# The gate and up projections of a feed-forward layer, token-major in blocks of 512 columns

## The chip, the cores and the metric

The kernel runs on one core of one Trainium2 chip. The metric is the device time of one execution in microseconds; the time before is the median of three runs.

## The reference

One decoder layer on 256 tokens of width 2,048 in float32. The two feed-forwards are what the change is about:

```python
def swiglu(x, w_gate, w_up, w_down):
    return (jax.nn.silu(x @ w_gate) * (x @ w_up)) @ w_down

x = x + 0.5 * swiglu(rms_norm(x, ffn1_norm), ffn1_w_gate, ffn1_w_up, ffn1_w_down)
...                                   # the token mixing, between the two
x = x + 0.5 * swiglu(rms_norm(x, ffn2_norm), ffn2_w_gate, ffn2_w_up, ffn2_w_down)
```

Gate and up weights are 2,048 x 5,632, down weights 5,632 x 2,048. `rms_norm` divides each token by the root of its mean square and multiplies by a gain per feature.

## The kernel before, in words

**Numbers in two halves.** A float32 value is used as a high part, rounded to the matmul's format (`whi`, `XH`), and a remainder (`wlo`, `XL`). A product is three terms: high x high, high x remainder, remainder x high.

**Weight tiles.** All weights come as tiles of 128 x 1,024 elements, 512 KB, one transfer each, through four `raw` buffers on SyncE's queue (`ensure_dma`, L286). ScalarE makes the high part (`split_hi`, L303), VectorE the remainder (`split_lo`, L322), each into four buffers, three tiles ahead of TensorE. A raw buffer is free, and the next transfer starts, when the remainder is made.

**Units.** A `Unit` is one bank pair of results: its tiles, the matmuls of half a tile (`emit`), and what follows (`done`). There are two forms. `unit_a` (L353) is feature-major: the weights are the stationary operand, 256 output columns, four 128-row slices of the contraction per tile. For each 128 columns it streams high and remainder of the activations together (512 columns) and then the high part alone (256), 16 matmuls to a tile. `unit_b` (L341) is token-major: the activations are the stationary operand, 512 output columns, two slices per tile, 12 matmuls of 512 columns. In the kernel before only the mixing stage uses `unit_b`.

**Feed-forward before.** `ffn` (L456) makes 22 gate units and 22 up units of 256 columns, alternating, then the down units, which read `H`, the product in two halves, feature-major. The normalisation's scale per token, R, is not known when the first units begin, since the gain alone is put into `XH` and `XL`; so the first two gates and ups are stored and scaled in jobs that wait for R. Each result leaves its bank by `fold` (a ScalarE copy and a VectorE addition); the gate is multiplied by R in a row (`RB`) and goes through Silu; the product with up is cast and its remainder taken.

**Order.** All engines run in the order written. Two units fit in the banks at once. Small work is in generators, the jobs: after each half tile `step` (L216) runs the jobs that are ready by a clock of estimated costs (`Estimate`), and `force` (L263) writes out the rest of a job at once. The main loop is at L1258.

**Opening.** The first gate and the first up unit are interleaved tile by tile. Their tiles share the x slices, which are loaded, scaled and split (`x_load`, `x_part`) just ahead of use; the first tile goes in pieces (`PIECES`).

Of the kernel before, what the change touches and what calls it, by code (L numbers as in the profile page):

```python
# [9 lines left out]
F32 = mybir.dt.float32  # L10
# [3 lines left out]
AF = mybir.ActivationFunctionType  # L14
# [4 lines left out]
S = 256  # L19
D = 2048  # L20
FF = 5632
EPS = 1e-6
NEG = -1e30
KD = D // 128
# [1 line left out]
NB = 4  # L26
NRAW = 4
LAG = 4.0
PIECES = ((0, 1), (1, 2), (2, 4))
SPREAD = ("ca", "R0", "R1", "R2")  # L30
MARGIN = 0.3

# [82 lines left out]
def layer(ctx: ExitStack, tc: tile.TileContext, xt, cols, w_small, b_in,  # L115
          wg1, wu1, wd1, w_in, cw1k, cw2k, cw1v, cw2v, wb_n, wb_m, w_out, wg2, wu2, wd2, out):
    nc = tc.nc
    est = Estimate()
    V, A, T, G = (Engine(e, n, est) for e, n in ((nc.vector, "V"), (nc.scalar, "A"), (nc.tensor, "T"), (nc.gpsimd, "G")))
# [10 lines left out]
    def nm(p):  # L130
        uid[0] += 1
        return f"{p}{uid[0]}"
# [20 lines left out]
    XH, XL = XX[:, :, 0, :], XX[:, :, 1, :]  # L153
# [29 lines left out]
    cur = {}  # L183
# [7 lines left out]
    def job(gen, name=None, need=(), rank=0):  # L191
        jobs.append([est.end, gen, name, need, rank])
        jobs.sort(key=lambda j: j[4])
# [69 lines left out]
    def force(name):  # L263
        settle()
        while name not in past:
            j = next(j for j in jobs if j[2] == name)
            for n in j[3]:
                force(n)
            if step(j):
                uptake(j)  # L270
# [15 lines left out]
    def ensure_dma(n):  # L286
        while state["dma"] <= min(n, len(tiles) - 1):
            i = state["dma"]
            src, nk, ncol = tiles[i]
            r = st.tile([128, nk, ncol], F32, name=nm("raw"), tag="raw", bufs=NRAW)  # L290
            est.q["D"] = max(est.q["D"], done_at.pop(i - NRAW, 0.0)) + 1.45
            if i == 0:
                for a, b in PIECES:
                    x_load(a, b)
                    nc.sync.dma_start(r[:, a:b, :], src[:, a:b, :])
            else:
                if i in (2, 4, 6):
                    x_load(2 * i, 2 * i + 4)
                nc.sync.dma_start(r, src)
            raws[i] = r, est.q["D"] + 2.0  # L300
            state["dma"] += 1
# [38 lines left out]

    def unit_b(w, c0, H, L, kts, done, pre=None):  # L341

# [10 lines left out]
    def unit_a(w, c0, ncol, kts, act, done, pre=None):  # L353

        nk = 1024 // ncol

        def emit(ps, h, e, wh, wl):
            a = act()
            for k in range(e * nk // 2, (e + 1) * nk // 2):
                kt = nk * h + k  # L360
                for c in range(ncol // 128):
                    cs = slice(c * 128, c * 128 + 128)
                    mul(ps[:, c, :], wh[:, k, cs], a[:, kt].rearrange("p a t -> p (a t)"), start=kt == 0, stop=False)
                for c in range(ncol // 128):
                    cs = slice(c * 128, c * 128 + 128)
                    mul(ps[:, c, 0:S], wl[:, k, cs], a[:, kt, 0, :], start=False, stop=kt == kts - 1)
        return Unit(blocks(w, c0, ncol, kts), emit, done, pre)
# [22 lines left out]
    def fold(o, ps, c=2):  # L390

        A.copy(o, ps[:, 0:c, S:])
        V.tensor_add(o, ps[:, 0:c, 0:S], o)

    units = []
# [56 lines left out]
    def rb2():  # L452
        return RB[:, None, :].to_broadcast([128, 2, S])


    def ffn(wg, wu, wd, first, nxt, name):  # L456


        env = {}

        def open_pool():
            p = tc.tile_pool(name=nm("ffn"), bufs=1)
            env["pool"] = p
            env["p"] = cur["ffn"] = p.__enter__()
            env["H"] = env["p"].tile([128, KF, 2, S], F32R, name=nm("H"), tag="h")

        def close_pool():
            env["pool"].__exit__(None, None, None)

        def gate_done(c):  # L470
            def f(ps):
                if c in (2, 3):
                    force(first + "up%d" % (c - 2))
                g = env["p"].tile([128, 2, S], F32, name=nm("sg"), tag="sg", bufs=2)
                fold(g, ps)
                env["g", c] = g
                if c < 2:
                    job(later(gate, c), first + "gate%d" % c, (first,))
                else:
                    gate(c)  # L480
            return f

        def gate(c):
            g = env["g", c]
            V.tensor_mul(g, g, rb2())
            A.activation(g, g, AF.Silu)

        def up_done(c):
            def f(ps):
                h = env["p"].tile([128, 2, S], F32, name=nm("sh"), tag="sh", bufs=2)  # L490
                fold(h, ps)
                env["h", c] = h
                if c < 2:
                    job(later(up, c), first + "up%d" % c, (first + "gate%d" % c,))
                else:
                    up(c)
            return f

        def up(c):
            h = env["h", c]  # L500
            V.tensor_mul(h, h, env["g", c])
            H = env["H"][:, 2 * c:2 * c + 2]
            A.copy(H[:, :, 0, :], h)
            V.tensor_sub(H[:, :, 1, :], h, H[:, :, 0, :].bitcast(F32))

        def later(f, c):
            yield
            f(c)

        def down_done(c):  # L510
            return lambda ps: residual(env["p"], c, ps, True, nxt, name)

        for c in range(FF // 256):
            units.append(unit_a(wg, c * 256, 256, KD, the_x, gate_done(c), open_pool if c == 0 else None))
            units.append(unit_a(wu, c * 256, 256, KD, the_x, up_done(c)))
        for c in range(D // 256 - (nxt is None)):
            units.append(unit_a(wd, c * 256, 256, KF, lambda: env["H"], down_done(c)))
        if nxt is None:
            units.append(unit_last(wd, D - 256, 256, KF, lambda: env["H"], lambda ps, k: store_last(env["p"], ps, k)))
        return close_pool  # L520
# [655 lines left out]
    close1 = ffn(wg1, wu1, wd1, "R0", C_GM, "R1")  # L1176
    close_mix = mixing()
    n = len(units)
    close2 = ffn(wg2, wu2, wd2, "R2", None, None)
    first2 = units[n].pre  # L1180

    def pre2():
# [1 line left out]
        first2()  # L1184
    units[n].pre = pre2

    units[0].guest, units[0].between = units.pop(1), (1, 3, 5, 7)
    plan = []
    for u in units:
        order = [u] * len(u.tiles)  # L1190
# [10 lines left out]
    x_at = {}  # L1201
    xv = xt.rearrange("(k p) t -> p k t", p=128)

    def x_load(a, b):
        nc.sync.dma_start(X[:, a:b, :], xv[:, a:b, :])  # L1205
        est.q["D"] += 0.36 * (b - a)
        for kt in range(a, b):
            x_at[kt] = est.q["D"] + 2.0
# [11 lines left out]
    for t in range(2):  # L1220
        G.affine_select(mcb[:, t, :], mcb[:, t, :], [[-16, 32]], OP.is_ge, NEG, base=128 * t - 31, channel_multiplier=1)
        G.affine_select(m01[:, t, :], m01[:, t, :], [[-16, 32]], OP.is_ge, 0.0, base=128 * t - 31, channel_multiplier=1)

    def x_part(a, b):
        est.after(x_at[a])
        for kt in range(a, b):
            A.activation(XH[:, kt, :], X[:, kt, :], AF.Identity, scale=col(C_G1 + kt))
            V.scalar_tensor_tensor(XL[:, kt, :], X[:, kt, :], col(C_G1 + kt), XH[:, kt, :].bitcast(F32),
                                   op0=OP.mult, op1=OP.subtract)

    def g_start():
        for a in range(8):
            yield
            v = X[:, 2 * a:2 * a + 2, :]
            if a == 0:
                A.activation(acc, v, AF.Square)
            else:
                sq = cur["ffn"].tile([128, 2, S], F32, name=nm("sq"), tag="y", bufs=2)
                A.activation(sq, v, AF.Square)
                V.tensor_add(acc, acc, sq)  # L1240
            yield
        yield from g_r()

    def open_x():
        ensure_split(0)
        ensure_split(1)
        x_part(4, 8)
        ensure_split(2)
    first = units[0].pre

# [8 lines left out]
    for h, (u, i) in enumerate(plan):  # L1259
        if i == 0:  # L1260
            if u.pre:
                u.pre()
            banks[u] = (u.bank or psA)()
        ps = banks[u]
        if h in (1, 3):
            x_part(6 + 2 * h, 10 + 2 * h)
        wh, wl, t, _ = splits.pop(h)
        est.q["T"] = max(est.q["T"], t)
        for e in range(2):
            u.emit(ps, i, e, wh, wl)  # L1270
            late = None if small_ones else cur.get("late")
            j = step()
            (split_lo if e else split_hi)(h + NB - 1)
            if u.mid and not e and i == len(u.tiles) - 1:
                est.after(est.q["T"] + 0.1)
                u.mid(ps)
            if e and i == len(u.tiles) - 1:
                del banks[u]
                est.after(est.q["T"] + 0.1)
                u.done(ps)  # L1280
            if late and late is cur.get("late"):
                settle()
            if j:
                uptake(j)
# [61 lines left out]
```

## Time and profile before

| | |
|---|---|
| median of 3 runs | 2225.91 us (2225.1 to 2227.18) |
| the profiled execution | 2226.1 us, its span 2224.4 us |
| TensorE busy | 2211.5 us (99%) |
| VectorE busy | 1373.9 us (62%) |
| ScalarE busy | 1104.7 us (50%) |
| mean transfer rate | 185 GB/s |

The span is the part between the first and the last instruction. Busy shares are means over the span. Matmuls overlap in the records, so the pace of the stream is read from the starts of matmuls, not from their lengths.

### The profile page before, as it was taken

The page shows a single profiled execution, that of the slowest core. Times are in us where ns is not written, and L with a number is a line of the kernel's source. Part 1 is how long each engine was busy: PE and PEld are TensorE (multiplying, and loading weights), DVE is VectorE, ACT ScalarE, POOL GpSimd, SP SyncE. Part 2 cuts the span into 40 slices and gives each one's busy share as a digit, 9 for nine tenths or more (in the row PEclk, how much of TensorE's full clock was granted, in tenths as well). Part 3 has the DMA queues.
Part 4 walks back from the last instruction along what each step waited for, and adds up shares of the span by engine and source line. Part 5 has one row for each costly group of instructions (what it writes and reads, how often), then busy time and mean ns, then how long its engine had stood idle before and what let it go on. Part 6 is the DMA issues. An engine that isn't in the chain of part 4 may idle for free.

```text
span 2224.4 us, 31821 instructions
## 1 busy us (share of the span) xinstructions
PE 2211.5 (99%) x12649; PEld 1913.9 (86%) x12649; DVE 1373.9 (62%) x1719; ACT 1104.7 (50%) x1471; POOL 27.8 (1%) x54
## 2 busy tenths in 40 slices
PE   8999999999999999999999999999999999999999
PEld 7888888888888888777888888888888888888888
DVE  7655555555555678876777666765555555555553
ACT  6444444444444465666774544554444444443332
POOL 0000000000000000001100000000000000000000
PEclk9999999999999999999999999999999999999999
DMA  7666666666655776544556666566666666666663
GB/s 248 184 192 187 188 192 186 188 190 193 189 181 185 201 229 192 162 131 122 155 170 189 189 189 188 182 190 183 189 188 189 189 189 190 189 199 199 199 197 126
DMA packets 395078, 412.59 MB, mean 185 GB/s; under 512 B 13296, under 2 KB 375920, under 8 KB 394928
## 3 DMA queue, kind: packets, MB, share of 16 engines
q1 hardware_dynamic: 394064, 408.08, 59.5%
q0 software_dynamic: 720, 2.36, 0.4%
q8 instruction: 99, 1.62, 0.3%
q14 instruction: 51, 0.42, 0.1%
q10 hardware_dynamic: 144, 0.11, 0.0%
HBM read 408.40 MB, written 2.10 MB: 185 GB/s over the span
## 4 chain that ended last, share of the span: by engine, by line
PE 98%; DVE 1%; DMA 0%; ACT 0%; issue 0%; SPq 0%; DVEq 0%; ACTq 0%
PE mm L110 94%; PE sc L110 2%; PE tr L110 2%; DVE wlo L110 0%; DMA raw<-in_wg_dram 0%; DMA raw<-in_w_in_dram 0%; DVE nx L110 0%; DVE t L110 0%; DVE y L110 0%; ACT t L110 0%; ACT whi L110 0%; ACT kk L110 0%; DVE mo L110 0%; SPq L1205 0%; DVE rt L110 0%
## 5 line engine op out<-in xcount | busy, mean ns | idle before, releaser
L110 DVE TENSOR_TENSOR wlo<-raw,whi 128x1024 fp32r<-128x1024 f32 (+1 forms) x772 | 929.8, 1224 | 558.0 <-ACT whi L110 555.3
L110 PE MATMUL mm<-XX,whi 128*128 128x512 f32 x3600 | 1137.5, 397 | 5.7 <-DVE XX L110 4.7
L110 ACT CAST whi<-raw 128x1024 fp32r<-128x1024 f32 (+1 forms) x772 | 792.8, 1046 | 555.8 <-PE mm L110 444.2
L110 PEld LDWEIGHTS mm<-XX,wlo 128*128 128x128 f32 x3600 | 676.9, 188 | 161.0 <-DVE wlo L110 2.2
L110 PE MATMUL mm<-XX,wlo 128*128 128x256 f32 x3600 | 710.4, 278 | 0.3 <-DVE wlo L110 0.2
L110 PEld LDWEIGHTS mm<-XX,whi 128*128 128x128 f32 x3600 | 550.6, 189 | 7.3 <-ACT whi L110 6.0
L110 PE MATMUL mm<-H,whi 128*128 128x512 f32 (+1 forms) x1496 | 446.4, 382 | 0.5 <-DVE y L110 0.5
L110 PEld LDWEIGHTS mm<-H,wlo 128*128 128x128 f32 x1408 | 264.9, 188 | 58.6
L110 PE MATMUL mm<-H,wlo 128*128 128x256 f32 x1408 | 284.2, 278 | 0.0
L110 PEld LDWEIGHTS mm<-H,whi 128*128 128x128 f32 x1496 | 228.3, 189 | 0.7 <-DVE y L110 0.7
L110 PE MATMUL mm<-whi,XX 128*128 128x512 f32 x576 | 191.5, 399 | 0.0
L110 PEld LDWEIGHTS mm<-whi,XX 128*128 128x128 f32 x576 | 108.4, 188 | 21.7 <-issue 0.7
L110 PE MATMUL mm<-wlo,XX 128*128 128x512 f32 x288 | 113.7, 395 | 0.2 <-DVE wlo L110 0.2
L110 PE MATMUL mm<-M__10703,whi 128*128 128x512 f32 x256 | 79.8, 393 | 0.0
L110 ACT COPY sg<-mm 128x512 f32<-128x512 f32 x44 | 25.8, 587 | 84.3 <-PE mm L110 84.3
L110 ACT COPY sh<-mm 128x512 f32<-128x512 f32 x44 | 25.8, 587 | 82.8 <-PE mm L110 82.8
L110 DVE TENSOR_TENSOR sg<-mm,sg 128x512 f32<-128x512 f32 x44 | 30.4, 692 | 54.7 <-ACT sg L110 54.5
L110 DVE TENSOR_TENSOR sh<-mm,sh 128x512 f32<-128x512 f32 x44 | 30.4, 692 | 54.5 <-ACT sh L110 54.5
L110 PEld LDWEIGHTS mm<-wlo,XX 128*128 128x128 f32 x288 | 54.3, 189 | 9.9 <-DVE wlo L110 0.6
L110 ACT CAST H<-sh 128x512 fp32r<-128x512 f32 x44 | 27.3, 620 | 62.3 <-DVE sh L110 62.3
L110 ACT ACTIVATE sg<-sg 128x512 f32<-128x512 f32 x44 | 27.8, 632 | 60.2 <-DVE sg L110 60.2
L110 PEld LDWEIGHTS mm<-M__10703,wlo 128*128 128x128 f32 x256 | 48.1, 188 | 10.9
(190 smaller groups left out, 1185.6 us busy)
## 6 DMA issues: line engine op xcount, KB each, us to landing
raw<-in_wu_dram SPq DMA_DIRECT2D x176, 512.0 KB, 4.7
raw<-in_wd_dram SPq DMA_DIRECT2D x176, 512.0 KB, 4.5
raw<-in_wg_dram SPq DMA_DIRECT2D x175, 512.0 KB, 4.7
raw<-in_w_in_dram SPq DMA_DIRECT2D x168, 512.0 KB, 4.5
raw<-in_w_out_dram SPq DMA_DIRECT2D x32, 512.0 KB, 4.7
raw<-in_wb_n_dram SPq DMA_DIRECT2D x16, 512.0 KB, 5.2
raw<-in_wb_m_dram SPq DMA_DIRECT2D x16, 512.0 KB, 4.3
bias<-in_b_in_dram POOLq DMA_DIRECT2D x9, 256.0 KB, 3.8
```

The source lines that it names most:

```text
L110: return g(out, *a, **k)
```

## The change

Gate and up use `unit_b` with 512 columns, 11 units each, eight tiles to a unit. Results are token-major, so R is a scalar per partition: Silu reads the bank directly and scales there. VectorE multiplies the up bank by the gate into `h`. Then a job (`g_turn`) turns `h` to feature-major with 16 transposes of 32 x 32 blocks in four groups (`turn`), and the cast and the remainder write `H`. A job must be over before the next gate is taken from its bank; the last one is forced out with the second-last tile of the first down unit. The first pair is copied out of its banks unscaled and scaled in place when R is known. In the opening, x is loaded and split two slices at a time, and the units interleave over 16 tiles.

```diff
-PIECES = ((0, 1), (1, 2), (2, 4))
+PIECES = ((0, 1), (1, 2))
...
-                if i in (2, 4, 6):
-                    x_load(2 * i, 2 * i + 4)
+                if i in range(2, KD, 2):
+                    x_load(i, i + 2)
...
+    def turn(o, h, j):
+
+        ov_ = o.rearrange("p k (t q f) -> p t k q f", t=2, f=32)
+        hv = h.rearrange("p t (k q f) -> p t k q f", q=4, f=32)
+        for i in range(4):
+            V.transpose(ov_[32 * j:32 * j + 32, :, :, i, :], hv[32 * i:32 * i + 32, :, :, j, :])
...
         def gate_done(c):
             def f(ps):
-                if c in (2, 3):
-                    force(first + "up%d" % (c - 2))
-                g = env["p"].tile([128, 2, S], F32, name=nm("sg"), tag="sg", bufs=2)
-                fold(g, ps)
-                env["g", c] = g
-                if c < 2:
-                    job(later(gate, c), first + "gate%d" % c, (first,))
+                if c == 1:
+                    force(first + "up")
+                if c:
+                    force(name + "h%d" % (c - 1))
+                g = env["g", c] = env["p"].tile([128, 2, 512], F32, name=nm("sg"), tag="sg", bufs=1)
+                if c:
+                    gate(g, ps)
                 else:
-                    gate(c)
+                    A.copy(g, ps)
+                    job(later(gate, g, g), first + "gate", (first,))
             return f
...
-        def gate(c):
-            g = env["g", c]
-            V.tensor_mul(g, g, rb2())
-            A.activation(g, g, AF.Silu)
+        def gate(g, src):
+            for t in range(2):
+                A.activation(g[:, t, :], src[:, t, :], AF.Silu, scale=cur["R"][:, t:t + 1])
...
         def up_done(c):
             def f(ps):
-                h = env["p"].tile([128, 2, S], F32, name=nm("sh"), tag="sh", bufs=2)
-                fold(h, ps)
-                env["h", c] = h
-                if c < 2:
-                    job(later(up, c), first + "up%d" % c, (first + "gate%d" % c,))
+                h = env["p"].tile([128, 2, 512], F32, name=nm("sh"), tag="sh", bufs=1)
+                if c:
+                    up(c, h, ps)
                 else:
-                    up(c)
+                    A.copy(h, ps)
+                    job(later(up, c, h, h), first + "up", (first + "gate",))
             return f
...
-        def up(c):
-            h = env["h", c]
-            V.tensor_mul(h, h, env["g", c])
-            H = env["H"][:, 2 * c:2 * c + 2]
-            A.copy(H[:, :, 0, :], h)
-            V.tensor_sub(H[:, :, 1, :], h, H[:, :, 0, :].bitcast(F32))
+        def up(c, h, src):
+            V.tensor_mul(h, src, env["g", c])
+            job(g_turn(c, h), name + "h%d" % c)
+
+        def g_turn(c, h):
+
+            ht = env["p"].tile([128, 4, S], F32, name=nm("ht"), tag="sg", bufs=1)
+            H = env["H"][:, 4 * c:4 * c + 4]
+            for j in range(4):
+                yield
+                turn(ht, h, j)
+                yield
+            yield
+            A.copy(H[:, :, 0, :], ht)
+            V.tensor_sub(H[:, :, 1, :], ht, H[:, :, 0, :].bitcast(F32))
+            yield
...
-        for c in range(FF // 256):
-            units.append(unit_a(wg, c * 256, 256, KD, the_x, gate_done(c), open_pool if c == 0 else None))
-            units.append(unit_a(wu, c * 256, 256, KD, the_x, up_done(c)))
+        for c in range(FF // 512):
+            units.append(unit_b(wg, c * 512, XH, XL, KD, gate_done(c), None if c else open_pool))
+            units.append(unit_b(wu, c * 512, XH, XL, KD, up_done(c)))
...
-    units[0].guest, units[0].between = units.pop(1), (1, 3, 5, 7)
+    units[0].guest, units[0].between = units.pop(1), range(1, KD, 2)
...
-        x_part(4, 8)
+        x_part(2, 4)
...
-        if h in (1, 3):
-            x_part(6 + 2 * h, 10 + 2 * h)
+        if h in range(1, KD - 4, 2):
+            x_part(h + 3, h + 5)
```

The rest of the diff passes the second feed-forward a name for its jobs and lets the sum of squares of x (`g_start`) wait until its slices have been split.

## Rows read from the trace of the kernel before

**Rows 1.** The page, parts 1 and 2: busy time, clock in 40 slices.
```profile
PE 2211.5 (99%) x12649; PEld 1913.9 (86%) x12649; DVE 1373.9 (62%) x1719; ACT 1104.7 (50%) x1471; POOL 27.8 (1%) x54
...
PEclk9999999999999999999999999999999999999999
```
**Rows 2.** The page, part 4: the chain of waits, share by engine.
```profile
PE 98%; DVE 1%; DMA 0%; ACT 0%; issue 0%; SPq 0%; DVEq 0%; ACTq 0%
```
**Rows 3.** Timeline of TensorE in gate and up: start us, us, engine, what.
```profile
300.12 0.63 PE L110 MATMUL mm<-XX,whi 128*128 128x512 f32 x2
300.59 0.40 PE L110 MATMUL mm<-XX,wlo 128*128 128x256 f32 x2
...
311.27 0.62 PE L110 MATMUL mm<-XX,whi 128*128 128x512 f32 x2
```
**Rows 4.** Timeline of TensorE in the mixing stage, token-major form.
```profile
786.01 0.62 PE L110 MATMUL mm<-whi,XX 128*128 128x512 f32 x2
786.46 0.39 PE L110 MATMUL mm<-wlo,XX 128*128 128x512 f32 x1
...
797.57 0.62 PE L110 MATMUL mm<-whi,XX 128*128 128x512 f32 x2
```
**Rows 5.** Timeline of the first 22 us.
```profile
4.67 1.19 PE L110 MATMUL mm<-XX,whi 128*128 128x512 f32 x2 [4.67 <-DVE XX L110]
...
8.15 0.62 ACT L110 CAST whi<-raw 128x512 fp32r<-128x512 f32 x1 [1.19 <-DMA raw<-in_wg_dram]
...
10.28 1.04 ACT L110 CAST whi<-raw 128x1024 fp32r<-128x1024 f32 x1 [1.51 <-DMA raw<-in_wu_dram]
...
18.00 0.62 PE L110 MATMUL mm<-XX,whi 128*128 128x512 f32 x2
```
**Rows 6.** The chain of waits up to 60 us: start us, us, what.
```profile
43.48 0.34 PE sc L110 x4
...
49.95 0.44 PE sc L110 x4
```
**Rows 7.** Timeline of TensorE at the end of the first gate and up stage.
```profile
501.46 0.63 PE L110 MATMUL mm<-H,whi 128*128 128x512 f32 x2
```
**Rows 8.** Busy time in two stretches; the last columns are clock, DMA share, GB/s.
```profile
0.00:20.00 20.00, 14.24 (x60) 11.23 (x61) 11.29 (x19) 13.69 (x24) 2.53 (x18) 1.00 0.91 298
100.00:500.00 400.00, 400.00 (x2299) 349.01 (x2298) 234.58 (x234) 187.53 (x216) 0.00 (x0) 1.00 0.61 189
```
**Rows 9.** Groups of ScalarE by shape: busy us, mean ns, idle before.
```profile
L110 ACT CAST whi<-raw 128x1024 fp32r<-128x1024 f32 x769 | 791.4, 1048 | 554.7 <-PE mm L110 444.2 <-ACT whi L110 69.5 <-issue 22.4
...
L110 ACT ACTIVATE sg<-sg 128x512 f32<-128x512 f32 x44 | 27.8, 632 | 60.2 <-DVE sg L110 60.2
L110 ACT CAST H<-sh 128x512 fp32r<-128x512 f32 x44 | 27.3, 620 | 62.3 <-DVE sh L110 62.3
L110 ACT COPY sh<-mm 128x512 f32<-128x512 f32 x44 | 25.8, 587 | 82.8 <-PE mm L110 82.8
```
**Rows 10.** Groups of VectorE by shape, the same columns.
```profile
L110 DVE TENSOR_TENSOR wlo<-raw,whi 128x1024 fp32r<-128x1024 f32 x769 | 928.3, 1227 | 556.7 <-ACT whi L110 554.0 <-PE mm L110 1.9
...
L110 DVE TENSOR_TENSOR H<-sh,H 128x512 fp32r<-128x512 f32 x44 | 30.5, 693 | 30.2 <-ACT H L110 30.2
...
L110 DVE TENSOR_TENSOR vcz<-sc,mask 128x1024 f32<-128x1024 f32 x1 | 1.2, 1225 | 1.7 <-PE sc L110 1.7
...
L110 DVE COPY t<-tr 128x256 f32<-128x256 f32 x2 | 0.7, 415 | 0.0
L110 DVE TENSOR_TENSOR_SCAN t<-t,t 4x256 f32<-4x256 f32 x1 | 0.7, 680 | 0.1
```
**Rows 11.** Timeline of one tile's cast and remainder in gate and up.
```profile
309.19 1.05 ACT L110 CAST whi<-raw 128x1024 fp32r<-128x1024 f32 x1 [1.73 <-PE mm L110]
...
310.27 1.23 DVE L110 TENSOR_TENSOR wlo<-raw,whi 128x1024 fp32r<-128x1024 f32 x1 [1.55 <-ACT whi L110]
```
**Rows 12.** The chain of waits from 840 to 900 us.
```profile
866.49 2.36 DVE wlo L110 x2
868.87 4.61 DMA raw<-in_w_in_dram
```

More of the change, by code (lines that the diff above doesn't have):

```diff
@@ L506, in later @@
-        def later(f, c):
-            yield
-            f(c)
+                h = env["p"].tile([128, 2, 512], F32, name=nm("sh"), tag="sh", bufs=1)
+                if c:
+                    up(c, h, ps)
+                else:
+                    A.copy(h, ps)
+                    job(later(up, c, h, h), first + "up", (first + "gate",))
+            return f
+        def up(c, h, src):
[8 more added lines that the diff above has]
+                yield
+            yield
+            A.copy(H[:, :, 0, :], ht)
+            V.tensor_sub(H[:, :, 1, :], ht, H[:, :, 0, :].bitcast(F32))
+            yield
@@ L510, in down_done, with later, turned, f @@
+        def later(f, *a):
+            yield
+            f(*a)
+        def turned(u):
+            emit = u.emit
+            def f(ps, h, e, wh, wl):
+                if h == len(u.tiles) - 2:
+                    force(name + "h%d" % (FF // 512 - 1))
+                emit(ps, h, e, wh, wl)
+            u.emit = f
+            return u
         def down_done(c):
             return lambda ps: residual(env["p"], c, ps, True, nxt, name)
-        for c in range(FF // 256):
-            units.append(unit_a(wg, c * 256, 256, KD, the_x, gate_done(c), open_pool if c == 0 else None))
-            units.append(unit_a(wu, c * 256, 256, KD, the_x, up_done(c)))
+        for c in range(FF // 512):
+            units.append(unit_b(wg, c * 512, XH, XL, KD, gate_done(c), None if c else open_pool))
+            units.append(unit_b(wu, c * 512, XH, XL, KD, up_done(c)))
@@ L516, in ffn @@
         for c in range(D // 256 - (nxt is None)):
             units.append(unit_a(wd, c * 256, 256, KF, lambda: env["H"], down_done(c)))
+            if c == 0:
+                turned(units[-1])
         if nxt is None:
@@ L1178, in layer @@
     n = len(units)
-    close2 = ffn(wg2, wu2, wd2, "R2", None, None)
+    close2 = ffn(wg2, wu2, wd2, "R2", None, "R3")
     first2 = units[n].pre
@@ L1222, in layer @@
         G.affine_select(m01[:, t, :], m01[:, t, :], [[-16, 32]], OP.is_ge, 0.0, base=128 * t - 31, channel_multiplier=1)
+    split_x = [0]
     def x_part(a, b):
-        est.after(x_at[a])
+        split_x[0] = b
+        est.after(x_at[b - 1])
         for kt in range(a, b):
@@ L1232, in g_start @@
         for a in range(8):
+            while split_x[0] < 2 * a + 2:
+                yield
+                yield est.q["T"] + 1.5
             yield
```

## The prediction, made blind

> **What bounds the kernel now.** I read the page first. [...] A busy share says nothing about how fast the stream is, so I went on to the timeline of TensorE. What the reader is to see there is the distance between starts, not the lengths of the bars, which overlap.
>
> In the feed-forward gate and up stage four matmuls (two of 512 columns, two of 256) repeat from 300.12 to 311.27: 11.15 us for 16 repeats, 0.697 us each [rows 3]. A weight tile of 512 KB is four repeats, 16 matmuls: 2.787 us. The token-major form that the change puts there is already used by the mixing stage. In a stretch of that stage where nothing else is on TensorE, three matmuls of 512 columns repeat from 786.01 to 797.57: 11.56 us for 17 repeats, 0.680 us each [rows 4]. A tile is four of those, 12 matmuls: 2.720 us. Both tiles stream 6,144 columns; the one with fewer and longer matmuls takes 0.067 us less.
>
> **The change part by part.**
>
> *Matmul form.* A feed-forward has 44 gate and up units of 4 tiles, and after the change 22 units of 8: 176 tiles either way, 352 in both. 352 x 0.067 = 23.6 us less. To see whether 2.787 holds for the whole stage: the fourth tile starts at 18.00 [rows 5], 173 tiles follow, 482.1 us, and the small matmuls of the normalisation add 0.34 + 0.34 + 0.44 us (two of these pieces are shown) [rows 6]; the sum, 501.3, is where the down projection's first matmul stands, 501.46 [rows 7]. No wait hides in the stage, so the difference per tile is passed on in full.
>
> *Start.* Today the first tile needs four 128-row slices of x, and x and weights together fill the DMA engines (share 0.91 in the first 20 us) [rows 8]. The first matmul is at 4.67, but casts still wait for weights at 8.15 and 10.28; from the fourth tile, 18.00, the pace is steady [rows 5]. Projected back by three tiles of 2.787, the stream has an effective start of 9.64. Ahead of the weights cast at 8.15 lie 1,024 KB, ahead of those cast at 10.28 another 512 KB: 246 KB per us. After the change a tile needs two slices, so the second tile's weights end at 1,280 KB instead of 1,536: 8.15 + 256/246 = 9.2. Cast 1.05 [rows 9], remainder 1.23 [rows 10], then 11 of its 12 matmuls at 0.227: it ends near 14.0, and 14.0 less two tiles is 8.6. I take 1.1 us as the gain. Bounds: nothing, if the larger first pieces (256 KB for 128) delay the first cast by as much; 2.5 us, if nothing but the DMA order counted. Later x slices stand behind a wait for a free weight buffer on SyncE's queue, two slices per two tiles; they are asked for before the weights of the tile that needs them, several tiles ahead, so I cost that at nothing. If that cover were gone, a late x holds up ScalarE's next casts.
>
> *Bank drain.* Removed per 512 columns: four ScalarE copies of 0.587, two Silu of 0.632, two casts of 0.620, and ten VectorE operations of 0.69 (the H row stands for all five kinds) [rows 9, 10]: 4.9 us of ScalarE, 6.9 us of VectorE. Added: two Silu straight from the bank, about 0.63 each, one cast like the weights' 1.05, one product and one subtraction of 1,024 elements, 1.225 each [rows 9, 10], and 16 transposes. A gate bank is free after 1.3 us, an up bank after 1.2, instead of about 1.3; the next unit in that bank starts a whole unit later, so this is hidden either way. The first pair instead is copied out (about 1.05 each) and scaled later; in the interleaved opening the gate's bank is wanted again one tile, 2.7 us, after its copy can begin, and everywhere else eight tiles after, so this is hidden too.
>
> *Transposes.* No row shows one. The instruction moves 256 elements on each of 32 partitions. VectorE's copy of 256 elements out of a bank takes 0.415 us, and the slowest operation on 256 elements that the trace has, a scan, 0.680 [rows 10]. I take 0.415, as a one-input copy is the nearest row, and keep 0.68 for the range; anything faster than 0.415 changes nothing, as will be seen. [...]
>
> VectorE per 512 columns, 16 tiles: 16 x 1.227 + 6.9 = 26.5 us before (its busy time in the quiet 400 us, 234.58 us for nine such blocks, agrees [rows 8]); after, 19.6 + 2.45 + 16 x 0.415 = 28.7 of 43.5 us. So it stays off the path on average. What counts is the burst. Groups of four transposes go out one per tile, each ahead of that tile's remainder (wlo), and the in-order engine makes wlo wait. How much lateness is covered: ScalarE casts a tile as soon as TensorE frees a buffer (309.19), the remainder starts at 310.27 [rows 11], and with four buffers TensorE reads it three tiles after the cast began, about 6 us after it is done. With the groups: counted from the end of an up unit, product 1.225, then after k tiles k x (4t + 1.227) us of VectorE, against a use at (k + 2) x 2.72 + 0.23. At the fourth, 16.55 against 6.13 + 16t: at t = 0.415 there are 3.8 us left, and TensorE starts to wait at t = 0.65. I cost the transposes at nothing. Beyond that each block loses 16 (t - 0.65), all 22 lose 352 (t - 0.65): 10.6 us at 0.68, and the whole gain of 24.7 at t = 0.72. The last block's transposes have nine down tiles, 25 us, before their result is read.
>
> *Sum.* 2226.1 (the profiled execution) - 23.6 - 1.1 = 2201.4 us. The median of the runs shown, 2225.9, is 0.2 below that execution, so no correction is worth making.
>
> **The rivals.**
>
> *VectorE becomes the bound (slower).* If a transpose takes over 0.72 us, the four-instruction groups push wlo past its use and the loss per block outgrows the gain. The price at 1.225, the time of a 1,024-element operation: 352 x 0.575 = 202, some 2404 us. For it speaks that a late remainder does reach TensorE today: around 866 the chain goes over two remainders and then over the transfer that waited for their buffers [rows 12]. Against it, no 256-element row is above 0.68. A milder case of the same, 0.66 to 0.70, gives 2205 to 2219.
>
> *Time goes by columns alone.* Both tiles have 6,144, so the form would be worth nothing and only the start remains: 2225.0. Against it are the two distances themselves, 0.348 us for 512 + 256 columns and 0.227 for 512 [rows 3, 4]: by columns the first would be 0.340. [...]
>
> *The token-major tile doesn't keep 2.72 here.* The quiet stretch is short, and in busier parts of the mixing stage the stream stalls on remainders and transfers [rows 12]. If such a hitch took a tenth of a microsecond on a third of the tiles, 12 us are lost: 2205 to 2219, 2213 in the middle. Against it: in this stage ScalarE has less to do than now, and the DMA share is 0.61 [rows 8].
>
> **How the numbers follow.** Forecast as summed 0.80; its own range is 2198 to 2204 (start 0 to 2.5 us, and 0.005 us on a tile, which the rounding of the rows leaves, 1.8 us). VectorE milder case 0.04, slower case 0.05. Columns alone 0.03. Hitches 0.06. Something that leaves no change at all 0.02. The predicted time is the likeliest, 2201.4. For the range I take 2197 to 2211: the forecast's own, and above it most of the hitch and mild cases; what is left out is the columns case, the slower case and the tails, under 2 in 10. About 0.2%, 4.5 us, is what a measurement of this kernel can tell from no change. Faster by more: 0.80 + 0.04 + 0.05 of the hitches' 0.06 = 0.89; within: 0.03 + 0.02 = 0.05; slower: the slower case and the last 0.01 of the hitches, should they be much longer, 0.06.
>
> **What would show it.** Token-major matmuls go from 864 to 5,088, their starts 0.227 apart all through the stage; the first matmul on H comes near 488.6 instead of 501.46; 352 transposes of about 0.42 us on VectorE; no wait of TensorE for wlo after the first ten tiles; the chain still 98% TensorE. The fourth tile starts near 16.7. I would be wrong if transposes stand above 0.65 us with wlo in the chain, if the distance of starts in the new stage is above 0.23, or if an x slice ends ScalarE's idle time after the first tiles.

## The result, and the profile after

The changed kernel takes 2201.03 us, median of four runs (2200.59 to 2201.35); the kernel before, run beside it on the same chip, 2226.29 (2225.1 to 2227.18). The ratio is 0.9889, 95% interval 0.9876 to 0.9901. Forecast were 2201.4 us and a range of 2197 to 2211.

The page of the kernel after, parts 1 and 4, against [rows 1, 2]:

```profile
span 2199.3 us, 29100 instructions
...
PE 2187.1 (99%) x11241; PEld 1850.3 (84%) x11241; DVE 1430.5 (65%) x1894; ACT 1068.7 (49%) x1364; POOL 27.8 (1%) x54
...
PE 97%; DVE 1%; DMA 0%; ACT 0%; issue 0%; SPq 0%; DVEq 0%; ACTq 0%
```

The span is 25.1 us shorter and TensorE is still busy for 99% of it: the same engine sets the time, with a faster stream. VectorE's busy time rose by 57 us, ScalarE's fell by 36, and neither shows in the chain.

Timeline of TensorE in the kernel after: a stretch of gate and up, against [rows 3], and the change to the down projection, against [rows 7]:

```profile
300.34 0.62 PE L110 MATMUL mm<-whi,XX 128*128 128x512 f32 x2
300.79 0.39 PE L110 MATMUL mm<-wlo,XX 128*128 128x512 f32 x1
...
311.22 0.61 PE L110 MATMUL mm<-whi,XX 128*128 128x512 f32 x2
...
488.24 0.62 PE L110 MATMUL mm<-H,whi 128*128 128x512 f32 x2
```

From 300.34 to 311.22 there are 16 repeats of three matmuls, 0.680 us each, so a tile takes 2.720 us: the pace that the mixing stage showed [rows 4]. The first matmul on `H` stands at 488.24 instead of 501.46, 13.2 us earlier; the second feed-forward brings the rest.

Groups of the kernel after, by engine and shape (busy us, mean ns, idle time before them), against [rows 9, 10]:

```profile
L110 PE MATMUL mm<-whi,XX 128*128 128x512 f32 x3392 | 1060.8, 391 | 4.9 <-ACT whi L110 4.9
L110 PE MATMUL mm<-wlo,XX 128*128 128x512 f32 x1696 | 663.1, 391 | 0.5 <-DVE wlo L110 0.5
...
L110 DVE STREAM_TRANSPOSE ht<-sh 32x256 f32<-32x256 f32 x352 | 153.6, 436 | 6.4
L110 DVE TENSOR_TENSOR H<-ht,H 128x1024 fp32r<-128x1024 f32 x22 | 26.8, 1218 | 1.1 <-ACT H L110 1.1
L110 DVE TENSOR_TENSOR sh<-mm,sg 128x1024 f32<-128x1024 f32 x20 | 24.5, 1224 | 8.2 <-PE mm L110 8.2
...
L110 ACT ACTIVATE sg<-mm,R 128x512 f32<-128x512 f32 x40 | 25.4, 686 | 33.0 <-PE mm L110 31.6 <-DVE H L110 1.4
L110 ACT CAST H<-ht 128x1024 fp32r<-128x1024 f32 x22 | 23.2, 1055 | 10.8 <-DVE ht L110 10.8
```

There are 3,392 + 1,696 = 5,088 token-major matmuls, as expected, and 352 transposes of 0.436 us. The last row but one already names something to come back to: Silu waits 1.4 us for VectorE's write of `H`.

Waits of TensorE in the kernel after (us in total, times, longest), and busy time in the two stretches of [rows 8] (the second one ends 20 us earlier, as the stage does):

```profile
PE mm L110 <- ACT whi L110: 4.9, 1, 4.9
...
PE mm L110 <- DVE wlo L110: 0.7, 3, 0.3
```

```profile
0.00:20.00 20.00, 14.85 (x53) 11.56 (x54) 11.98 (x18) 14.14 (x22) 2.53 (x18) 1.00 0.89 299
100.00:480.00 380.00, 380.00 (x1678) 314.78 (x1677) 252.04 (x298) 167.01 (x167) 0.00 (x0) 1.00 0.65 193
```

The wait of 4.9 us is the first matmul's. For remainders TensorE waits three times, 0.7 us in all, and never between 30 and 700 us. VectorE is busy for 252 of 380 us (66%).

Timeline of VectorE over one block of the kernel after, from the product to the write of `H`:

```profile
227.32 1.22 DVE L110 TENSOR_TENSOR sh<-mm,sg 128x1024 f32<-128x1024 f32 x1 [0.41 <-PE mm L110]
228.58 1.78 DVE L110 STREAM_TRANSPOSE ht<-sh 32x256 f32<-32x256 f32 x4
230.39 1.22 DVE L110 TENSOR_TENSOR wlo<-raw,whi 128x1024 fp32r<-128x1024 f32 x1
...
237.80 1.79 DVE L110 STREAM_TRANSPOSE ht<-sh 32x256 f32<-32x256 f32 x4
239.62 2.36 DVE L110 TENSOR_TENSOR wlo<-raw,whi 128x1024 fp32r<-128x1024 f32 x2
```

The reader sees the burst that the prediction counted: four groups of four transposes, each ahead of one remainder, back to back. The fourth remainder ends at 239.62 + 1.23 = 240.85, 13.53 us after the product began. TensorE reads it six tiles after the unit's first remainder, which it reads at 227.35: 227.35 + 6 x 2.72 = 243.67, which is 16.35 us after the product began. So 2.8 us of cover are left in a usual block.

### The profile page after: what moved, and what is told of

It is laid out like the page before. It is cut to its first block, busy times and chain, and to the rows that moved or that the text cites. A ratio compares the mean times of both kernels' runs of the same rounds, so it can differ in the third digit from the quotient of the medians.

```text
span 2199.3 us, 29100 instructions
## 1 busy us (share of the span) xinstructions
PE 2187.1 (99%) x11241; PEld 1850.3 (84%) x11241; DVE 1430.5 (65%) x1894; ACT 1068.7 (49%) x1364; POOL 27.8 (1%) x54
## 4 chain that ended last, share of the span: by engine, by line
PE 97%; DVE 1%; DMA 0%; ACT 0%; issue 0%; SPq 0%; DVEq 0%; ACTq 0%
PE mm L110 94%; PE sc L110 2%; PE tr L110 2%; DVE wlo L110 0%; DMA raw<-in_wu_dram 0%; DMA raw<-in_w_in_dram 0%; DVE nx L110 0%; DVE t L110 0%; DVE y L110 0%; ACT t L110 0%; ACT whi L110 0%; ACT kk L110 0%; DVE mo L110 0%; DVE rt L110 0%; DVE kk L110 0%
## 5 line engine op out<-in xcount | busy, mean ns | idle before, releaser
L110 PE MATMUL mm<-whi,XX 128*128 128x512 f32 x3392 | 1060.8, 391 | 4.9 <-ACT whi L110 4.9
L110 PEld LDWEIGHTS mm<-whi,XX 128*128 128x128 f32 x3392 | 638.1, 188 | 136.2 <-ACT whi L110 4.9
L110 PE MATMUL mm<-wlo,XX 128*128 128x512 f32 x1696 | 663.1, 391 | 0.5 <-DVE wlo L110 0.5
L110 PEld LDWEIGHTS mm<-wlo,XX 128*128 128x128 f32 x1696 | 319.2, 188 | 66.0 <-DVE wlo L110 1.8
L110 PE MATMUL mm<-XX,whi 128*128 128x512 f32 x784 | 249.6, 399 | 0.0
L110 PEld LDWEIGHTS mm<-XX,wlo 128*128 128x128 f32 x784 | 147.1, 188 | 34.8 <-DVE wlo L110 0.9
L110 DVE STREAM_TRANSPOSE ht<-sh 32x256 f32<-32x256 f32 x352 | 153.6, 436 | 6.4
L110 PE MATMUL mm<-XX,wlo 128*128 128x256 f32 x784 | 155.7, 278 | 0.2 <-DVE wlo L110 0.2
L110 PEld LDWEIGHTS mm<-XX,whi 128*128 128x128 f32 x784 | 120.6, 189 | 1.2 <-issue 0.2
L110 PE MATMUL mm<-M__10001,whi 128*128 128x512 f32 x256 | 79.9, 393 | 0.0
L110 PE MATMUL mm<-O__5735,whi 128*128 128x512 f32 x128 | 40.3, 396 | 0.0
L110 PE MATMUL mm<-h__8408,whi 128*128 128x512 f32 x128 | 40.0, 394 | 0.0
```

What stands on the lines that cost most here:

```text
L110: return g(out, *a, **k)
```

## The experiments

Two theories stood against each other from the start. *Form*: fewer and longer matmuls stream the same columns faster, and the transposes lie behind other work. *Rivals*: the gain comes from elsewhere (the start, relieved ScalarE), or the transposes already cost something and the form gives more than the sum shows. Beside the experiments the kernel before took 2225.4 to 2225.7 us (medians), beside the change 2226.3, so a difference from the change is known to about 1 us from the times alone.

**Half of it undone.** The second feed-forward keeps its gate and up in the old form, with the functions that drained its banks before (not shown).

```diff
-        for c in range(FF // 512):
...
+        for c in range(FF // 256 if nxt is None else 0):
+            units.append(unit_a(wg, c * 256, 256, KD, the_x, old_gate_done(c), open_pool if c == 0 else None))
+            units.append(unit_a(wu, c * 256, 256, KD, the_x, old_up_done(c)))
+        for c in range(FF // 512 if nxt is not None else 0):
...
```

> The second feed-forward keeps its gate and up units feature-major with 256 columns, the first is changed with the opening. Theory (0.067 us on every one of 352 tiles, and the opening): half of the tiles lose their gain, 176 x 0.067 = 11.8 us, so about 2212.8 us, and the first matmul on H still comes near 488.2 us. Rival (most of the gain comes from the opening and from x being spread over 16 tiles): within 3 us of the changed kernel, about 2201 to 2204.

Measured: 2213.27 us (2212.97 to 2213.77), ratio to before 0.9943 (0.9927 to 0.9960). That is 12.2 us above the whole change, half of its gain; 176 x 0.067 = 11.8 was asked of one feed-forward. The gain goes by the tiles in this form and not by the opening, which this kernel shares.

**Columns in shorter matmuls.** The token-major form stays, but all except the first and the last matmul of each accumulation are cut into two of 256 columns: the same columns, the same engines' work around them, 4,048 matmuls more.

```diff
-                    mul(ps[:, t, :], H[:, kt, ts], wh[:, k, :], start=kt == 0, stop=False)
...
+                    for a, x, start, stop in ((H, wh, kt == 0, False), (H, wl, False, False), (L, wh, False, kt == kts - 1)):
+                        for cs in (slice(0, 256), slice(256, 512)) if halves and not start and not stop else (slice(0, 512),):
+                            mul(ps[:, t, cs], a[:, kt, ts], x[:, k, cs], start=start, stop=stop)
...
```

> In the token-major gate and up units all but the first and last accumulating matmul of each result half are split into two of 256 columns: 188 matmuls per unit instead of 96, the columns unchanged. Theory (a matmul costs its columns plus a fixed 13 to 14 ns; 256 columns then take 0.120 us, as in the last unit of the kernel before, where 155 take 18.61 us): 184 x 0.120 + 4 x 0.227 = 22.99 us per unit for 21.76, 44 units, 54 us more: about 2255. Rival (time goes by columns alone): 2201, no change. In between, if a matmul of 256 columns takes the 0.115 us that it takes among longer ones in the feature-major tile: 2214.

Measured: 2254.77 us (one run), 53.7 above the whole change. Timeline of TensorE of this kernel:

```profile
299.81 0.64 PE L110 MATMUL mm<-whi,XX 128*128 128x256 f32 x4
300.29 0.40 PE L110 MATMUL mm<-wlo,XX 128*128 128x256 f32 x2
300.53 0.64 PE L110 MATMUL mm<-whi,XX 128*128 128x256 f32 x4
```

Six matmuls of 256 columns start every 0.72 us, 0.120 each, where three of 512 take 0.680, 0.2267 each. Two halves cost 0.240, 0.0133 more than the whole, and 4,048 x 0.0133 = 54 us. This settles the rival by which time goes by columns alone. The two distances also give the parts: 256 columns more take 0.1067 us, 2.4 columns per ns at a granted clock of 1.00, and some 13 ns come with every matmul.

The number of matmuls does not explain the whole 0.067 us of a tile. By these figures the four matmuls of the old form would take 2 x 0.2267 + 2 x 0.120 = 0.693 us, and they took 0.697: in that mixed stream the two of 512 columns stand 0.47 us and not 0.453 [rows 3], the two of 256 columns 0.23 instead of 0.24. So 4 x 0.0133 = 0.053 us per tile, 19 of the 23.6 us, come from the number of matmuls; the rest, some 5 us, goes with the mix of the two lengths, and no run here shows why.

**No transposes.** The 352 transposes are left out, so `H` holds the right work in the wrong places.

```diff
-            ht = env["p"].tile([128, 4, S], F32, name=nm("ht"), tag="sg", bufs=1)
+            ht = h.rearrange("p t (a b) -> p (t a) b", b=S)
...
-                turn(ht, h, j)
```

> The 352 transposes are left out: H is written from the token-major product without being turned, so the numbers in H are in the wrong places; cast and remainder have the same size as before. Theory (VectorE's 153.6 us of transposes lie wholly beside TensorE): 2201, within 0.5 us. Rival (the bursts cost something that the gain of the form conceals): faster by the part that they cost, 2 us or more.

Measured: 2200.59 us (one run). VectorE's busy time between 100 and 480 us falls from 252 to 190 of 380 us:

```profile
100.00:480.00 380.00, 380.00 (x1678) 314.66 (x1677) 189.98 (x157) 165.73 (x168) 0.00 (x0) 1.00 0.65 194
```

154 us of work on VectorE are worth 0.4 us of time, and not even that is theirs: the fourth tile begins 0.5 us earlier in this run (15.7 for 16.2), and so does the first matmul on `H` (487.73 for 488.24). Between the two both kernels take 472.0 us. The transposes are hidden.

**How far the cover reaches.** Two kernels repeat some transposes, writing the same result, without the planner's knowledge, so that the order of everything else stays. The first repeats two of each group of four (24 instead of 16 in a block), the other all (`i < 4`, 32).

```diff
             V.transpose(ov_[32 * j:32 * j + 32, :, :, i, :], hv[32 * i:32 * i + 32, :, :, j, :])
+            if i < 2:
+                nc.vector.transpose(ov_[32 * j:32 * j + 32, :, :, i, :], hv[32 * i:32 * i + 32, :, :, j, :])
```

> Half of the transposes are done twice, the second time not counted by the planner: six instructions to a group, 0.654 us per block of work for 0.436, right at the point from which TensorE should wait. Theory (lateness counted as in the prediction, 352 (t - 0.65)): 1.4 us more at most, 2201 to 2203. Rival (VectorE hides far more than that account says): 2201, and no wait for wlo. Other rival (the limit lies lower than 0.65): 2205 or more.

> Every transpose is done twice, the second time without being counted by the planner, so that the groups still go out one per tile but take twice as long: 0.87 us per block of work for 0.436. Theory (the prediction's account of lateness: nothing up to 0.65 us, then 16 (t - 0.65) per 512 columns): 352 x 0.22 = 78 us more, about 2279, with wlo in the list of what TensorE waits for. Rival (VectorE has room on average, 36 of 43.5 us per 512 columns, and four buffers hide the burst): about 2201.

Measured: 2227.13 and 2323.75 us (one run each), 26.1 and 122.7 above the change. Both come out above what was expected. Timeline of VectorE in the kernel with half of them repeated, from its block's product to the fourth remainder:

```profile
234.77 1.22 DVE L110 TENSOR_TENSOR sh<-mm,sg 128x1024 f32<-128x1024 f32 x1 [0.41 <-PE mm L110]
...
250.83 2.36 DVE L110 TENSOR_TENSOR wlo<-raw,whi 128x1024 fp32r<-128x1024 f32 x2
```

and of TensorE, where that remainder is read:

```profile
250.66 0.61 PE L110 MATMUL mm<-whi,XX 128*128 128x512 f32 x2
252.11 0.50 PE L110 MATMUL mm<-wlo,XX 128*128 128x512 f32 x1 [0.83 <-DVE wlo L110]
252.44 0.63 PE L110 MATMUL mm<-whi,XX 128*128 128x512 f32 x2
```

After 250.66 two matmuls 0.227 apart should be followed by the next at 251.11, again 16.35 us after the product began; the remainder ends at 250.83 + 1.23 = 252.06 and the matmul starts at 252.11, 1.0 us late. The start behind it is 0.33 away instead of 0.227, and the next few lose a little more: the whole tile takes 3.867 us, 1.147 more than 2.720. The products of two blocks start 44.67 us apart, and 43.52 after the change: the same 1.15, in each of eighteen blocks, 20.6 us. The first block of the first feed-forward loses 4.3, that of the second 0.5, and each down projection, in which the last block's transposes stand, 0.5; an opening 0.3 us earlier takes some of it back. Together that is the 26.1 us. So the mechanism of the "VectorE becomes the bound" rival is real, and its point was put too high: a transpose takes its place on VectorE for 0.455 to 0.465 us with the gap behind it, not for its own 0.436, and the other operations of a block take 13.53 - 16 x 0.455 = 6.25 us, not 6.13, against a deadline of 16.35, not 16.55. By these the wait begins at t = (16.35 - 6.25) / 16 = 0.63 us instead of 0.65; 24 repeats spaced 0.46 stand for t = 0.69, which makes 16 x (0.69 - 0.63) = 1.0 us late, as measured.

With all of them repeated, 32 spaced 0.46 stand for t = 0.92, and the same account asks for 16 x (0.92 - 0.63) = 4.6 us a block. Eleven of the eighteen usual blocks lose 4.9, but seven lose 6.5, and the first of the first feed-forward 8.2 (the second's 4.4, the two down projections 5.8 and 4.3). What the seven have besides is a lower clock. Timeline of TensorE behind the last late remainder of such a block, and busy time in two stretches (the column before the DMA share is the granted clock):

```profile
420.21 0.50 PE L110 MATMUL mm<-wlo,XX 128*128 128x512 f32 x1 [1.96 <-DVE wlo L110]
...
422.09 0.63 PE L110 MATMUL mm<-wlo,XX 128*128 128x512 f32 x1
422.52 1.05 PE L110 MATMUL mm<-whi,XX 128*128 128x512 f32 x2
423.37 0.63 PE L110 MATMUL mm<-wlo,XX 128*128 128x512 f32 x1
```

```profile
421.30:424.60 3.30, 3.30 (x9) 2.57 (x8) 3.30 (x3) 0.57 (x1) 0.00 (x0) 0.50 0.89 270
100.00:500.00 400.00, 374.35 (x1571) 300.76 (x1571) 289.95 (x406) 153.76 (x155) 0.00 (x0) 0.97 0.57 172
```

TensorE stands waiting for 26 of 400 us there. After two waits of 1.93 and 1.96 us (at 415.23 and 420.21) its granted clock is 0.50 for a while (from 421.30 to 424.60 in the stretch shown), and three matmuls take 1.28 us instead of 0.68: this block loses 1.6 us more. In fifteen of the eighteen blocks the clock falls behind such a wait. In eight of them it falls ahead of the last late remainder; there the matmuls run slower but the next wait is 0.4 us instead of 1.9, and the block still loses 4.9. So the clock cost 7 x 1.6 = 11 us in these blocks; its part in the first ones and in the down projections was not separated. After the change the clock is 1.00 in the whole stage; with half of the transposes repeated it fell once, in the first block.

**The same work, planned.** Again every transpose twice, but both counted by the planner, which then spaces the groups to VectorE's load.

```diff
             V.transpose(ov_[32 * j:32 * j + 32, :, :, i, :], hv[32 * i:32 * i + 32, :, :, j, :])
+            V.transpose(ov_[32 * j:32 * j + 32, :, :, i, :], hv[32 * i:32 * i + 32, :, :, j, :])
```

> Every transpose is done twice and the planner counts both, so that it spaces the groups wider, about two tiles apart. VectorE's work is the same as with the uncounted doubling. Theory (only the burst matters, not VectorE's sum): two tiles give 5.44 us for 2 x 1.23 + 8 x 0.436 = 5.95, half a microsecond late per group, 2 us in four groups, less than what is covered: 2201 to 2203. Rival (VectorE's sum matters, or the unfinished groups that are forced out at the next gate do): 2210 or more.

Measured: 2220.56 us (one run), 19.5 above the change. Spacing brings most of the 122.7 back, but the expectation fell. Timeline of ScalarE of this kernel around the end of a gate unit, and its waits over the whole span:

```profile
216.29 1.05 ACT L110 CAST H<-ht 128x1024 fp32r<-128x1024 f32 x1 [2.68 <-DVE ht L110]
219.88 1.26 ACT L110 ACTIVATE sg<-mm,R 128x512 f32<-128x512 f32 x2 [2.53 <-DVE H L110]
221.03 3.89 ACT L110 CAST whi<-raw 128x1024 fp32r<-128x1024 f32 x4
```

```profile
ACT H L110 <- DVE ht L110: 71.4, 20, 10.1
...
ACT sg L110 <- DVE H L110: 48.6, 20, 2.8
```

A job that isn't over by the end of the next gate unit is written out at once, ahead of that gate's Silu, because the turned block lies in the gate's buffer. ScalarE then waits for the turned block, and again for `H`, with the casts of four tiles queued behind; they run back to back from 221.03, and the remainders come late. A usual block loses some 0.5 us (44.05 from product to product, for 43.52), 18 times; the first feed-forward's first block loses 7.8, the second's 1.5. In the first block TensorE waits 4.9 us for a cast, and its granted clock is 0.50 from 86.3 to 93.0, so a part of the 7.8 is the clock's. The theory that this leaves: most of the time is lost not by VectorE's load, but by the forced end's place in ScalarE's queue.

**The forced end moved.** To test that: the same doubled transposes, but the turned block has a buffer of its own, and the job is forced only at the end of the up unit, before its product. To make room, `y` has one buffer instead of two in the feed-forwards.

```diff
...
@@ gate_done
-                if c:
-                    force(name + "h%d" % (c - 1))
@@ up_done
+                if c:
+                    force(name + "h%d" % (c - 1))
@@ g_turn
-            ht = env["p"].tile([128, 4, S], F32, name=nm("ht"), tag="sg", bufs=1)
+            ht = env["p"].tile([128, 4, S], F32, name=nm("ht"), tag="ht", bufs=1)
...
```

> The doubled and counted transposes once more, but the turned block has a buffer of its own (it shared the gate's) and has to be over only when the next up unit is drained, eight tiles later than before; to make room, the small residual buffer is single in the feed-forwards. Theory after the runs so far (the 19.5 us that doubling cost came from the transposes being forced out ahead of the next gate's Silu, behind which ScalarE's casts then stood): 2201 to 2205, and ScalarE no longer waits before Silu for the remainder of H. Rival (VectorE is simply too late with the remainders of the weights while groups go out): 2212 or more, with TensorE waiting for wlo.

Measured: 2204.17 us (one run), 3.1 above the change, where the same VectorE work had cost 19.5. Busy time in the stretch, the waits of ScalarE between 60 and 480 us, and those of TensorE's weight loads (PEld) between 30 and 480:

```profile
100.00:480.00 380.00, 380.00 (x1672) 312.80 (x1671) 310.69 (x442) 164.86 (x167) 0.00 (x0) 1.00 0.62 192
```

```profile
ACT whi L110 <- PE mm L110: 180.9, 113, 1.7
ACT whi L110 <- DMA raw<-in_wu_dram: 34.1, 17, 2.6
ACT sg L110 <- PE mm L110: 16.0, 10, 1.7
ACT whi L110 <- DVE wlo L110: 6.4, 5, 1.3
```

```profile
PEld mm L110 <- DVE wlo L110: 2.4, 9, 0.3
```

VectorE is busy for 311 of 380 us (82%) and in this stretch no matmul waits. Neither the wait for the turned block nor Silu's wait for `H` is there any more, and the first blocks lose nothing. What is left of the cost belongs to the rival: once in each block a weight load of TensorE waits 0.27 us for a remainder behind the groups, and the block takes 43.68 us instead of 43.52, eighteen times 0.155, 2.8 of the 3.1 us. The buffer and the later place were changed together; which of them alone would do was not tried.

**x four slices at a time.** The loads of x go back to four slices each after the first two; splitting them stays two at a time.

```diff
-                if i in range(2, KD, 2):
-                    x_load(i, i + 2)
+                if i == 1:
+                    x_load(2, 4)
+                if i in (2, 4, 6):
+                    x_load(2 * i, 2 * i + 4)
```

> Only the order of loads at the start is undone: x comes four slices at a time again, as in the kernel before, so 256 KB more lie ahead of the second tile's weights. Theory (the second tile's weights set the start, 246 KB per us): 1.0 us later, the fourth tile at 17.2 us instead of 16.2, about 2202.0 us. Rival (the start gains by the larger transfers or by one piece less on the queue, not by the order of x): fourth tile at 16.2, 2201.0.

Measured: 2201.85 us (2201.68 to 2202.10), ratio to before 0.9893 (0.9877 to 0.9910). The median is 0.8 above the change's, near the 1.0 expected, but the two were set against different runs of before and the intervals of their ratios overlap. The fourth tile starts at 16.8 us here, at 16.2 after the change, and between 15.7 and 17.0 in seven other kernels of this section whose opening is that of the change (the one with shorter matmuls left out). This experiment settles nothing below 1 us.

**The form carried further.** If it is the form that pays, it should pay in the down projection too: 1,536 of its 2,048 columns become token-major units, and their results are scaled, turned back by the same `turn` and added to X in jobs.

```diff
...
-        for c in range(D // 256 - (nxt is None)):
-            units.append(unit_a(wd, c * 256, 256, KF, lambda: env["H"], down_done(c)))
+        for c in range(3):
+            units.append(unit_b(wd, c * 512, lambda: env["H"], None, KF, wide_done(c)))
...
+        for c in range(6, D // 256 - (nxt is None)):
+            units.append(unit_a(wd, c * 256, 256, KF, lambda: env["H"], down_done(c)))
...
```

> The changed kernel, and besides the first 1,536 of the 2,048 columns of both down projections are computed token-major in blocks of 512 as well, turned back by 16 transposes each and added to x in jobs; the last 512 columns stay as they are. 66 tiles in each feed-forward change their form. Theory (0.067 us for each such tile, wherever the drain is hidden): 132 x 0.067 = 8.8 us less than the changed kernel, 2192.2 us. Rival (with H as the stationary operand, or with the residual in jobs, the tile doesn't reach 2.72 us): 2196 to 2206.

Measured: 2192.60 us (2191.73 to 2192.74), ratio to before 0.9851 (0.9836 to 0.9865): the fastest version here, 8.4 us below the change, where 132 tiles x 0.067 = 8.8 were asked. Timeline of TensorE in its down projection:

```profile
599.86 0.62 PE L110 MATMUL mm<-whi,H 128*128 128x512 f32 x2
600.31 0.39 PE L110 MATMUL mm<-wlo,H 128*128 128x512 f32 x1
...
603.26 0.62 PE L110 MATMUL mm<-whi,H 128*128 128x512 f32 x2
```

From 599.86 to 603.26 there are five repeats of three matmuls, every 0.68 us again, in a third stage.

## Why the prediction was right, and where its terms were off

**Matmul form: right.** 23.6 us were forecast, from the distance of starts in a stage where the form already ran. The new tile takes 2.720 us as there, undoing half of it costs half, and shorter matmuls of the same columns cost what was expected of them (53.7 us for 54). The forecast needed only the two distances; the reason that it named beside them, fewer and longer matmuls, covers some four fifths of the difference. The first matmul on `H` came at 488.24 (forecast 488.6). The rival with hitches, by which the pace of the quiet mixing stretch might not hold here, is gone: TensorE waits for no remainder between 30 and 700 us.

**Start: right in kind, 1.1 forecast, 1.6 in this profile.** Timeline of the first 18 us of the kernel after, against [rows 5]:

```profile
8.52 1.04 ACT L110 CAST whi<-raw 128x1024 fp32r<-128x1024 f32 x1 [2.00 <-DMA raw<-in_wu_dram]
...
16.00 0.62 PE L110 MATMUL mm<-whi,XX 128*128 128x512 f32 x2
```

The fourth tile begins with the second matmul of the last row, 16.2 (forecast 16.7); less three tiles of 2.72 the effective start is 8.06 instead of 9.64. The second tile's weights are cast at 8.52, where the forecast had them land at 9.2. The rate in that forecast was misread a little: the two casts shown are 2.13 us apart, and 512 KB in 2.13 us are 240 KB per us, not 246, which moves the landing by 0.02 us only. With the eight starts of one opening between 15.7 and 17.0, this term is known as 0.8 to 2.1 us (against the one profile of the kernel before), so 1.1 was not wrong, but less sharp than its digit. 23.6 + 1.6 = 25.2 us, beside 25.1 of the spans; an agreement to 0.1 us is luck with a start that varies by 1.3.

**Bank drain: right.** In gate and up no bank ends a wait of TensorE, and behind the first tiles no x slice one of ScalarE; ScalarE lost 36 us of work, but TensorE had not waited for it before either (400 of 400 us busy in [rows 8]).

**Transposes: hidden as forecast, with less in hand than forecast.** Taken at 0.415 us from a copy, they are 0.436, and 0.455 from start to start. 0.436 is 5% above the copy, which has 256 elements on each partition too. The cover of a usual block is 2.8 us, not 3.8, since 16 x 0.04 us of transposes with their gaps, 0.1 us of other operations and a deadline 0.2 us earlier were not in the sum. Where the wait begins is 0.63 us and not 0.65, and the loss beyond it has another 0.15 us per block, which the late tile takes to come back to pace.

**What the sum did not look at.** It counted a usual block, from the end of an up unit. The thinnest place is the first block of the first feed-forward, where the first pair's scaling waits for R and its turn is forced out ahead of the next gate's Silu. Timeline of the kernel after there, ScalarE, then VectorE, then TensorE:

```profile
76.81 1.05 ACT L110 CAST H<-ht 128x1024 fp32r<-128x1024 f32 x1 [3.48 <-DVE ht L110]
79.22 1.27 ACT L110 ACTIVATE sg<-mm,R 128x512 f32<-128x512 f32 x2 [1.35 <-DVE H L110]
80.38 3.89 ACT L110 CAST whi<-raw 128x1024 fp32r<-128x1024 f32 x4
...
81.45 4.63 DVE L110 TENSOR_TENSOR wlo<-raw,whi 128x1024 fp32r<-128x1024 f32 x4 [2.33 <-ACT whi L110]
...
83.19 0.39 PE L110 MATMUL mm<-wlo,XX 128*128 128x512 f32 x1
```

It is the pattern of the doubled and planned transposes, once: ScalarE stands for 3.48 and 1.35 us with four casts behind it, the first remainder ends at 81.45 + 1.23 = 82.68, and TensorE reads it at 83.19. Only 0.5 us were left. Slower transposes cost time there first and most, by a wait in ScalarE's queue that no rival named: with half of them repeated this block lost 4.3 us (a part of it at the lower clock) and a usual one 1.15.

## What to carry to other kernels

When one engine is busy all the time, compare the distance between starts of the forms that the kernel already runs: fewer, longer matmuls of the same columns paid the forecast amount in gate and up (0.067 us a tile) and again in the down projection (8.4 us where 8.8 were asked). Work moved to an engine with room was free here only where each burst of it ended before the next operand was due (16 transposes to a block cost nothing, 24 cost 1.15 us), so count the burst with its gaps against the deadline, and look for the block where it is forced out instead of spread. Look also at where a late job is forced out, and whose buffer it holds until then: with a buffer of its own and a later forced end (not tried one by one), twice the transposes cost 3.1 us instead of 19.5.

## What was not expected of the hardware

In streams of one length behind the opening every matmul cost some 13 ns beyond its columns at a granted clock of 1.00 (0.2267 us for 512, 0.120 for 256, the columns at the 2.4 per ns that these two give), each with a weight load of its own (11,241 of both in the kernel after). Where the clock was granted at 0.50, matmuls of 512 columns started 0.427 us apart (1.28 us for three, all transposes repeated). Half of the 2.4 columns per ns, an estimate from the two distances, gives 0.427 for the columns alone and leaves nothing for the 13 ns. That pace also stood without a lower clock in the record: in the opening of the kernel after, starts from 6.21 to 8.78 stand 0.428 us apart with no wait between them, at a recorded 1.00. After a wait of 0.83 us TensorE's next starts were slower than its pace, the first 0.33 us away instead of 0.227, some 0.15 us lost in all (half of the transposes repeated); with the forced end moved, blocks with a weight load 0.27 us late lost as much, 0.155. With all transposes repeated, a block in which the clock fell ahead of the last late remainder lost 4.9 us, as the three without a lower clock did; where it fell behind that remainder, 1.6 us more. With VectorE busy for 82% of a stage TensorE lost 0.155 us a block, while at 72% (290 of 400 us, all transposes repeated without a plan) it lost 4.9 and more: in these two runs not the share decided, but the place of the work.
